# adaLN's remaining groups after both mixers, and the state-space recurrence over chunks on VectorE

## The chip, the core and the metric

The kernel runs on one core of a Trainium2 chip. The core has five engines that each work through a queue of their own, in order: TensorE (PE in the profile; its weight loads are PEld), VectorE (DVE), ScalarE (ACT), GpSimd (POOL) and SyncE (SP), which here issues nearly all transfers. The metric is the device time of one execution in microseconds.

## The reference

One layer of a streaming encoder for 512 tokens of width 2048, all in 32-bit floats:

```python
mod = (silu(c) @ w_ada + b_ada)                      # 2048 -> 6 x 2048
sh_m, sc_m, g_m, sh_f, sc_f, g_f = split(mod, 6)
h = layer_norm(x) * (1 + sc_m) + sh_m
u, q, k, v, z, beta, a, gate_s, gate_g = split(h @ w_in)
y_s = s5_mixer(u, ...) @ w_up_ssm                    # 64 groups x 16 channels, 64 complex states each
y_g = gated_deltanet(q, k, v, z, beta, a, ...) @ w_up_gdn   # 8 heads, chunks of 64 tokens
m = sigmoid(gate_s) * y_s + sigmoid(gate_g) * y_g
x = layer_norm(alpha * x + g_m * (m @ w_out), ln1_g, ln1_b)
h = layer_norm(x) * (1 + sc_f) + sh_f
x = layer_norm(alpha * x + g_f * swiglu(h), ln2_g, ln2_b)
```

The state-space mixer (S5) is a linear recurrence over the tokens. The delta-rule mixer (gated DeltaNet, "gd") goes head by head and, inside a head, chunk by chunk.

## The kernel before

**Stages.** PE runs one main line of matrix products: the input tiles for u, then for each of eight heads its q, k, v and z tiles with two gate tiles ahead of each head but the first, the remaining gate tiles, the GLU, the two up projections (merge), the output projection in two token halves, and the feed-forward layer in groups of 8 hidden tiles. Each weight block of 512 KB is loaded by SP into `raw` (three buffers), split by ACT into `whi` and by DVE into `wlo` (both 32-bit in a form PE multiplies in one pass), and each product is three PE instructions: high by high, high by low, low by high.

**Side lines.** The mixers, the adaLN sums and the LayerNorms are Python generators woven into the main line by `Order`: it keeps a rough price for each instruction, and after each triple of products (`tick`) it emits the next piece of any side line whose inputs should be there by then. Only the order of each engine's queue comes of this; on the chip each engine waits for what its next instruction needs. Where the main line can't go on, `until(...)` emits pieces of the side lines with no products between. The places used below: ahead of the tiles of head h it asks for `heads_done >= h - 1`; at the end of the output projection it drains the first half's LayerNorm line.

**The state-space mixer** (`s5_batch`, eight batches). POOL makes tables V and H (names s_V, s_W, s_H), PE makes the chunks' contributions, ACT brings them to `St` (s_S), and then the recurrence over chunks runs in `cstep`: 14 steps of four dependent POOL instructions in each batch, seven of them on 64 columns and seven on 8. POOL then adds the carried states (s5wf), and PE forms the output from s_K and s_H (px_s).

**The delta-rule mixer.** `gdn_prep` makes a head's decays on POOL and ACT (g_G, g_E, g_ET); `gdn_solve` inverts its triangular matrix on PE and DVE (g_T, g_X, g_TT), walks over four pairs of chunks (vn, St), and closes the head: squares on ACT, so on DVE, ro on POOL, g_th on DVE, then four closing transposes on PE (px_gd<-cst,g_th).

**adaLN.** The shift and scale of the first LayerNorm are made at the start. The other four vectors are `ada_rest()`: 16 groups of 512 columns, each 16 loads of 256 KB (SP) and 16 multiply-adds into `aacc` on DVE, then a few small products on PE (px_ada). The line is added as soon as the heads' conv weights are there, so it runs beside the mixers, and it only takes DVE when `Order` holds DVE for free. `ada_line` also has a second form, used when the buffers of `P2` exist, that is, after the mixers: five of the 16 products go to ACT, four sums to POOL into `aacc2`, and one more DVE sum joins the two. With `ada_deep` six loads are in flight instead of four. In this kernel all 16 groups are emitted before `P2` exists.

`switch()` waits for both mixers, frees their memory and opens `P2` (pools bp and q2); it runs between two pairs of gate tiles. The gate row for the output projection (`ada_m`, 4 groups), the columns for the second LayerNorm (`ada_f`, 12 groups) and the last row (`ada_done`, 16 groups) are asked for later.

Of the kernel before, what the change touches and what calls it, by code (L numbers as in the profile page):

```python
# [16 lines left out]
PSUM = bass.MemoryType.PSUM  # L17
# [19 lines left out]
def shape_constants():  # L37
    """128-wide masks, then masks of 64 x 64 diagonal blocks, stacked twice over the partitions."""
    i = np.arange(128)[:, None]
    j = np.arange(128)[None, :]  # L40
    m = [np.eye(128), j < i, i <= j, i // 16 == j // 16]
    i, j = i % 64, np.arange(64)[None, :]
    pair = (i // 2 == j // 2)
    m += [i == j, -1.0 * (pair & (j < i)), -1.0 * (pair & (i < j))]
    m += [(i // b == j // b + 1) & (i // b % 2 == 1) for b in (2, 4, 8, 16, 32)]
    return np.concatenate([a.astype(np.float32) for a in m], axis=1)
# [10 lines left out]
class Order:  # L57
    """Emission order of all engines: a main line of matrix products with side lines woven in.

    A rough model of the engines tells when each result is there, so that a side line's next piece is emitted  # L60
    about when its inputs are.
    """
    LAT = 0.12
# [12 lines left out]
    def _first(self, ap):  # L76
        """When the slot of a tile that is written for the first time gets free."""
        t = ap.tensor
        nm = ap.name
        if nm in self.ready or not hasattr(t, "tag_meta") or t.tag_meta is None:  # L80
            return 0.0
        q = self.slots.setdefault(t.tag, [])
        q.append(nm)
        n = t.tag_meta.bufs
        return self.last.get(q[-n - 1], 0.0) + self.LAT if len(q) > n else 0.0
# [73 lines left out]
class Engine:  # L159
    """An engine's instructions, with their rough price told to the order."""  # L160

# [110 lines left out]
def s5_setup(k, p, lam_re, lam_im, log_dt):  # L272
    """Powers of the discretised poles and their B factors, in [(re|im, state), group] and [(group parity, state), pair]."""
    nc, v, act, pool, pe = k.nc, k.v, k.act, k.pool, k.pe
# [98 lines left out]
def s5_batch(k, j, prm, d_col):  # L373
    """One tile of 128 channels (8 groups): u^T comes from k.du, 2 * gelu(y)^T goes to k.dz."""
    v, act, pool, pe, ld = k.v, k.act, k.pool, k.pe, k.ld
    b_re, b_im, c_re, c_im = prm
    s, t = k.s5, k.t5
# [84 lines left out]
    def cstep(dst, prev, rr, rs, n):  # L462
        x = w1[:, :, :, 0:n]
        shp = [128, 4, 2, n]
        for src, cf_ in ((prev, bc(rr.unsqueeze(2).unsqueeze(3), shp)), (prev[:, :, ::-1], bc(rs.rearrange("p r q -> p q r").unsqueeze(3), shp))):
            pool.tensor_tensor(out=x, in0=src, in1=cf_, op=M)
            pool.tensor_tensor(out=dst, in0=dst, in1=x, op=A)
    a8r, a8s = s.R8[:, 0, 0, q0:q0 + 4], s.R8s[:, :, q0:q0 + 4]
# [59 lines left out]
def gdn_setup(k, p, psb, a_log, dt_bias, conv_w, norm_w):  # L528
    """psb rows 0..7: beta logits, rows 8..15: decay logits, over tokens."""
    v, act, pool, pe, ld = k.v, k.act, k.pool, k.pe, k.ld  # L530
# [76 lines left out]
def gdn_conv(k, h, which, ps):  # L607
    """Causal convolution over tokens, out of PSUM."""
    s = k.gd
    a = k.tg("qkv"[which])  # L610
    col = lambda w: s.cw[:, 24 * w + 8 * which + h:24 * w + 8 * which + h + 1]
    k.act.activation(a, ps, AF.Identity, scale=col(3))
    for w in (2, 1, 0):
        d = 3 - w
        k.v.scalar_tensor_tensor(out=a[:, d:512], in0=ps[:, 0:512 - d], scalar=col(w), in1=a[:, d:512], op0=M, op1=A)
    return a
# [21 lines left out]
def gdn_prep(k, h):  # L638
    """All of a head that does not wait for the chunks before: decays, norms, the strictly lower matrix, q k^T."""
    v, act, pool, pe = k.v, k.act, k.pool, k.pe  # L640
# [106 lines left out]
def gdn_solve(k, h, r):  # L747
    """The inverse of the unit lower matrix by doubling blocks, then the chunks' recurrence and the head's output."""
    v, act, pool, pe = k.v, k.act, k.pool, k.pe
# [136 lines left out]
class Weights:  # L886
    """The stream of weight blocks, loaded and split into two float32r parts ahead of their use."""

# [63 lines left out]
    def poll(self):  # L952
        """The next block's load, once its slot is free."""
        i = self.loaded
# [7 lines left out]
def kernel(ctx, tc, x, c, w_ada, b_ada, w_in, lam_re, lam_im, log_dt, b_re, b_im, c_re, c_im,  # L962
# [39 lines left out]

# [1 line left out]
    ws = Weights(k, wpool)  # L1004
# [47 lines left out]

# [1 line left out]
    cst = cpool.tile([128, 128], F32, name="cst")  # L1054
# [18 lines left out]
    def by_pos(a):  # L1073
        """A tile whose tokens are ordered by their position in the chunk first, read in the tokens' order."""
        return a.rearrange("p (s c) -> p c s", s=8)

# [1 line left out]
    def split(hi, lo, src, eng=None):  # L1078
# [8 lines left out]
    def after(first):  # L1087
        """Between products: the next block's split and the side lines."""
        if first:
            ws.run_ahead()  # L1090
        o.tick()
# [11 lines left out]
    def gemm2(kt, acts, done, pre=None):  # L1103
        """Two neighbouring 128-column tiles, K in blocks of 8 slices."""
        pss = [psum_mm(), psum_mm()]
# [17 lines left out]
    def ada_line(p, col0):  # L1123
        """Per-partition partial sums of 512 adaLN columns."""
        acc = p.tile([128, 512], F32, name="aacc", tag="aacc", bufs=1)
# [34 lines left out]
    def ada_cols_line(p, j, q, dst, plus):  # L1160
        """512 columns of adaLN vector j, as columns."""
        acc = yield from ada_line(p, 2048 * j + 512 * q)
# [6 lines left out]
    def ada_row_line(p, j, q):  # L1169
        """Half of 512 columns of adaLN vector j, to a row in DRAM."""  # L1170
        acc = yield from ada_line(p, 2048 * j + 512 * q)
# [10 lines left out]

# [1 line left out]
    hT = []  # L1184
# [158 lines left out]

# [1 line left out]
    adp = ctx.enter_context(pool_of(name="adp", bufs=1, side="right"))  # L1345
# [15 lines left out]

# [1 line left out]
    gps, sps = ExitStack(), ExitStack()  # L1363
# [32 lines left out]
    o.until(lambda: k.cw_ready)  # L1396
    o.add(ada_rest())
    gate_next = iter(range(0, 32, 2))
# [7 lines left out]
    for h in range(8):  # L1406
# [9 lines left out]
        k.heads[h, 3] = z  # L1416
# [1 line left out]
    def switch():  # L1418
        """The mixers' memory becomes the operands' of the later products."""
        o.drain(s5l)  # L1420
# [22 lines left out]
        k.ada_deep = True  # L1443
        o.add(operands())

    def bt(dtype=F32R):
# [17 lines left out]

# [1 line left out]
    k.ada_deep = False  # L1466
# [62 lines left out]
    def row_of(src, q):  # L1529
        """A quarter of a row of 2048, on all partitions."""  # L1530
        return row_to(P2[1].tile([128, 512], F32, name="grow", tag="grow", bufs=1), src, q)
# [4 lines left out]

# [1 line left out]
    xa = [[None] * 4 for _ in range(4)]  # L1538
    h2 = [[None] * 16 for _ in range(2)]

    def ln_stats(st):
        """Mean, rstd and -mean * rstd of a token tile, as columns."""
        mv = cpool.tile([128, 2], F32, name="mv", tag="mv", bufs=4)
# [13 lines left out]
    def affine(r, st, g, b, how):  # L1557
        """((r - mean) * rstd) * g + b, in place; how: 0 on DVE, 1 shared, 2 without DVE."""
        if how == 0:
# [7 lines left out]
    def ln_half(hf, new_big):  # L1567
        """LN1, then LN0 with the FFN's adaLN, for 256 tokens; alpha * x1 stays in xa, h2^T goes to h2[hf]."""
        rows = []
# [84 lines left out]

# [1 line left out]

    def ffn_tile(gsj, hs):
        """2 * silu(gate) * up of one hidden tile, for the token halves hs."""
        pss = []
# [25 lines left out]
    def scaled(t, q, ps, gf):  # L1685
        """Adds the second gate's row times a product to a tile of the residual."""
        tmp = t2("ld")
# [33 lines left out]

# [1 line left out]
    k.gf_rows += [row_to(bt(F32), drow[5], q) for q in range(2, 4)]  # L1723
# [71 lines left out]
```

## Time and profile before

| | |
|---|---|
| median of 3 runs | 3234.25 us (3231.43 to 3240.14) |
| span of the profiled execution | 3234.4 us |
| busy, PE / DVE / ACT / POOL | 96% / 49% / 29% / 27% |
| mean granted clock of PE | 0.973 |
| moved by DMA | 458.6 MB, 142 GB/s |

The profile is of one execution. Its span, from the first to the last instruction, is 3234.4 us; no other time of that execution is given, and the span lies within 0.2 us of the median. Each row of a group gives the engine, the operation, output <- inputs by the program's names, the shape, the count, then busy us and mean ns of one, then the idle time before it and what ended that. A row "PE a <- DVE b" says that PE waited, before an instruction that writes a, for DVE to write b. Nearly all elementwise code goes through one helper (L170), so groups are told apart by tile names.

Behind the mixers, by the table of stretches, come the gates, the GLU and the merge (to about 1520 us), the output projection with the first LayerNorm half (to about 1700 us) and the feed-forward layer.

### The profile page before, as it was taken

To read this page: it belongs to the slowest core of one execution; us is meant where nothing else is said; L and a number is where in the kernel's file an instruction comes from. 1 tells how busy PE (TensorE), PEld (TensorE's weight loads), DVE (VectorE), ACT (ScalarE), POOL (GpSimd) and SP (SyncE) were. 2 spreads that over 40 slices of the span, in tenths; PEclk is the share of its full clock that TensorE was granted. 3 is DMA by queue.
4 is the path that set the end of the run, shared out by engine and by line. 5 is a ranking of instruction groups with operands and counts; after the bars stand their busy time and mean duration, and the time that the engine had idled before them with its cause. 6 is when DMAs were issued, how large, how long until landed. Compare 5 with 4: busy or idle time off the path is not lost.

```text
span 3234.4 us, 47422 instructions
## 1 busy us (share of the span) xinstructions
PE 3093.7 (96%) x19409; PEld 2699.8 (83%) x19409; DVE 1596.2 (49%) x2023; ACT 923.6 (29%) x1306; POOL 871.3 (27%) x1125
## 2 busy tenths in 40 slices
PE   6899999988999999999999999999999999999997
PEld 3587777877777788888879999998998999899895
DVE  6546776756866432444677543333233333333327
ACT  3233332222232232322354532221221222222121
POOL 4747766656754100000031102002001100200202
PEclk8899999988999999999999999999999999999998
DMA  9655556545555244445767543333333333333333
GB/s 342 213 147 156 151 162 181 151 138 169 162 143 175 79 156 134 152 147 163 237 209 202 160 150 105 92 95 108 92 92 105 98 92 98 104 93 95 108 98 117
DMA packets 521754, 458.60 MB, mean 142 GB/s; under 512 B 56144, under 2 KB 403632, under 8 KB 521536
## 3 DMA queue, kind: packets, MB, share of 16 engines
q1 hardware_dynamic: 514336, 442.47, 44.9%
q10 hardware_dynamic: 7200, 13.10, 1.1%
q8 instruction: 152, 2.49, 0.3%
q14 instruction: 66, 0.54, 0.1%
HBM read 435.60 MB, written 19.89 MB: 141 GB/s over the span
## 4 chain that ended last, share of the span: by engine, by line
PE 69%; POOL 9%; issue 5%; DVE 5%; DMA 2%; ACT 2%; SPq 1%; POOLq 0%; DVEq 0%; ACTq 0%
PE pm L211 51%; PE px_fo L211 14%; POOL s_S L170 3%; POOL s5w L170 2%; PE px_gd L211 2%; DVE aacc L170 1%; PE px_s L211 1%; SPq L170 1%; DMA w<-in_w_ada_dram 1%; DVE wlo L170 1%; DVE at L170 1%; ACT whi L170 1%; POOL g_E L170 1%; POOL g_ET L170 1%; POOL s_H L170 0%
## 5 line engine op out<-in xcount | busy, mean ns | idle before, releaser
L170 DVE TENSOR_TENSOR wlo<-raw,whi 128x1024 fp32r<-128x1024 f32 x541 | 684.0, 1266 | 899.8 <-ACT whi L170 896.8
L211 PE MATMUL pm<-at,whi 128*128 128x512 f32 (+1 forms) x3200 | 986.2, 379 | 6.4 <-ACT whi L170 3.6
L211 PE MATMUL pm<-bt,whi 128*128 128x256 f32 (+1 forms) x5312 | 988.5, 291 | 0.3 <-ACT whi L170 0.3
L170 ACT CAST whi<-raw 128x1024 fp32r<-128x1024 f32 x541 | 566.1, 1048 | 1098.6 <-PE pm L211 538.9
L211 PEld LDWEIGHTS pm<-bt,whi 128*128 128x128 f32 x5312 | 800.9, 192 | 15.9 <-ACT whi L170 0.5
L211 PEld LDWEIGHTS pm<-at,whi 128*128 128x128 f32 x3200 | 591.2, 192 | 102.9 <-ACT whi L170 4.0
L211 PE MATMUL pm<-bt,wlo 128*128 128x256 f32 (+1 forms) x2656 | 632.1, 291 | 1.5 <-DVE wlo L170 1.5
L211 PE MATMUL pm<-at,wlo 128*128 128x512 f32 (+1 forms) x1600 | 594.9, 372 | 2.5 <-DVE wlo L170 2.5
L211 PEld LDWEIGHTS pm<-bt,wlo 128*128 128x128 f32 x2656 | 447.5, 192 | 9.5 <-DVE wlo L170 1.9
L170 POOL TENSOR_TENSOR at<-at,ld 128x512 f32<-128x512 f32 x80 | 120.5, 1537 | 1148.7 <-DVE ld L170 1148.7
L211 PEld LDWEIGHTS pm<-at,wlo 128*128 128x128 f32 x1600 | 306.5, 192 | 55.9 <-DVE wlo L170 3.3
L211 PE MATMUL px_fo<-whi,at 128*128 128x512 f32 x976 | 304.7, 389 | 1.7 <-ACT whi L170 1.7
L170 DVE SCALAR_TENSOR_TENSOR aacc<-w,ccol,aacc 128x512 f32<-128x512 f32 x240 | 217.5, 906 | 26.6 <-DMA w<-in_w_ada_dram 22.4
L211 PEld LDWEIGHTS px_fo<-whi,at 128*128 128x128 f32 x976 | 183.2, 188 | 39.9 <-ACT whi L170 2.1
L211 PE MATMUL px_fo<-wlo,at 128*128 128x512 f32 x488 | 190.0, 389 | 0.8 <-DVE wlo L170 0.8
L170 POOL TENSOR_TENSOR rs<-rs,mhalf 128x1 f32<-128x1 f32 (+1 forms) x13 | 11.4, 873 | 627.8 <-DVE rs L170 627.8
L170 POOL TENSOR_TENSOR s_S<-s_S,s5w 128x64 f32<-128x64 f32 (+1 forms) x224 | 106.9, 477 | 17.6
L211 PEld LDWEIGHTS px_fo<-wlo,at 128*128 128x128 f32 x488 | 91.7, 188 | 19.9 <-DVE wlo L170 1.1
L211 PE MATMUL pm<-whi,bt 128*128 128x512 f32 x320 | 103.2, 396 | 3.3 <-DVE at L170 3.3
L211 PE MATMUL px_fo<-whi,bt 128*128 128x512 f32 x320 | 101.8, 389 | 0.0
L170 DVE SCALAR_TENSOR_TENSOR gs<-gg,pm 128x512 f32<-128x512 f32 x36 | 24.7, 687 | 154.4 <-ACT gg L170 154.4
L170 DVE TENSOR_TENSOR gs<-gs,pm 128x512 f32<-128x512 f32 x36 | 24.7, 687 | 132.5 <-PE pm L211 132.5
(374 smaller groups left out, 3139.1 us busy)
## 6 DMA issues: line engine op xcount, KB each, us to landing
raw<-in_ffn_w_in_dram SPq DMA_DIRECT2D x208, 512.0 KB, 4.1
raw<-in_w_in_dram SPq DMA_DIRECT2D x146, 512.0 KB, 3.8
w<-in_w_ada_dram SPq DMA_DIRECT2D x256, 256.0 KB, 3.6
raw<-in_ffn_w_out_dram SPq DMA_DIRECT2D x88, 512.0 KB, 3.6
wad<-in_w_ada_dram SPq DMA_DIRECT2D x64, 512.0 KB, 5.6
raw<-in_w_mix_out_dram SPq DMA_DIRECT2D x64, 512.0 KB, 4.4
raw<-in_w_up_gdn_dram SPq DMA_DIRECT2D x16, 512.0 KB, 3.4
raw<-in_w_up_ssm_dram SPq DMA_DIRECT2D x16, 512.0 KB, 3.4
```

What stands on the lines that cost most here:

```text
L170: r = f(*a, **kw)
L211: r = self.e.matmul(out, **kw)
```

## The change

Two edits do something; all the others take comments and docstrings out.

```diff
@@ s5_batch, cstep
         for src, cf_ in ((prev, ...), (prev[:, :, ::-1], ...)):
-            pool.tensor_tensor(out=x, in0=src, in1=cf_, op=M)
-            pool.tensor_tensor(out=dst, in0=dst, in1=x, op=A)
+            v.tensor_tensor(out=x, in0=src, in1=cf_, op=M)
+            v.tensor_tensor(out=dst, in0=dst, in1=x, op=A)
@@ ahead of the loop over heads
     o.until(lambda: k.cw_ready)
-    o.add(ada_rest())
     gate_next = iter(range(0, 32, 2))
@@ switch()
         k.ada_deep = True
         o.add(operands())
+        o.add(ada_rest())
```

The 448 instructions of the recurrence (8 batches x 56) go from POOL's queue to DVE's. The adaLN groups start after `switch()`, so they now take `ada_line`'s second form. Because all side lines share one plan, the order moves in many other places too. Three of them follow.

PE's queue where head 0 ends, before: the four closing transposes stand among products of the main line (pm<-at), and so do the tables of the next state-space batch (px_s).

```order
L216 MATMUL px_s_3360<-cst,s_V 128x128 x4
L211 MATMUL px_s_3368<-s5Cs,s_V 128x128 x4
L211 MATMUL pm<-at,whi 128x512 x2
L211 MATMUL pm<-at,wlo 128x512
L211 MATMUL px_s_3386<-s5Cs,s_V 128x128 x4
L216 MATMUL px_gd<-cst,g_th 128x128 x4
L211 MATMUL pm<-at,whi 128x512 x2
L211 MATMUL pm<-at,wlo 128x512
```

The same place in PE's queue now, in two pieces: the last two chunk steps of head 0, and, after 16 small products of the state-space mixer (px_s<-s_U,s_K and px_s<-s_X,s_H in turn, of which the first and the last two are shown), the closing transposes.

```order
L211 MATMUL px_gd<-vn,g_kt 128x128
L211 MATMUL pm<-vn,g_ET 128x128
L211 MATMUL px_gd<-g_v,TTfull 128x128
L211 MATMUL px_gd<-St,g_wT 128x128
L211 MATMUL pm<-St,g_G 128x128
L211 MATMUL pm<-vn,g_ET 128x128
L211 MATMUL px_s_3170<-s_U,s_K 128x64
```

```order
L211 MATMUL px_s_3170<-s_U,s_K 128x64
L211 MATMUL px_s_3170<-s_X,s_H 128x64
L216 MATMUL px_gd<-cst,g_th 128x128 x4
L211 MATMUL px_gd<-g_T,g_MT 64x64 x8
L211 MATMUL pm<-at,whi 128x512 x2
L211 MATMUL pm<-at,wlo 128x512
```

No main product is left between the last chunk step and the transposes: this is the `until` ahead of the tiles of head 2, and the same holds, with zero, one or ten triples of products between, at the `until` ahead of each of the heads 3 to 7. Before, each head ended some way ahead of its `until`.

DVE's queue in the output projection's second half, before (at<-at,mv,gg and at<-at,rs,gs are the first LayerNorm's affine step, BN_STATS its statistics, pm<-pm,grow the gate row's product):

```order
L170 BN_STATS st<-at 128x6
L170 SCALAR_TENSOR_TENSOR at<-at,mv,gg 128x512
L170 SCALAR_TENSOR_TENSOR at<-at,rs,gs 128x512
L170 TENSOR_TENSOR wlo<-raw,whi 128x1024 x2
L170 BN_STATS st<-at 128x6
L170 TENSOR_TENSOR pm<-pm,grow 128x512
L170 SCALAR_TENSOR_TENSOR at<-at,pm 128x512
```

The same place in DVE's queue now:

```order
L170 SCALAR_TENSOR_TENSOR at<-at,mv,gg 128x512
L170 SCALAR_TENSOR_TENSOR at<-at,rs,gs 128x512
L170 SCALAR_TENSOR_TENSOR aacc<-w_12971,ccol,aacc 128x512
L170 TENSOR_TENSOR wlo<-raw,whi 128x1024
L170 SCALAR_TENSOR_TENSOR aacc<-w_12979,ccol,aacc 128x512
L170 TENSOR_TENSOR wlo<-raw,whi 128x1024
L170 SCALAR_TENSOR_TENSOR aacc<-w_13000,ccol,aacc 128x512
L170 TENSOR_TENSOR pm<-pm,grow 128x512
```

An adaLN multiply-add (aacc) now stands before most weight splits (wlo). By the order, about ten of the 16 groups end before the output projection, and the last ends in the first feed-forward tiles.

PE's queue where the output projection ends (pm<-whi,bt) and the feed-forward tiles begin (pm<-bt,whi, 256 columns), now:

```order
L211 MATMUL pm<-wlo,bt 128x512
L211 MATMUL pm<-whi,bt 128x512
L216 MATMUL px_tr<-cst,ld 128x128 x16
L211 MATMUL pm<-bt,whi 128x256 x2
L211 MATMUL pm<-bt,wlo 128x256
```

The 16 transposes (px_tr) are the last half of the first LayerNorm half's; before, all 32 stood in fours among the output projection's products, and the first feed-forward tile followed the last product directly. At the second half's end 16 stand in a row now, where 12 did before.

## The prediction

> **What bounds the kernel now.** I read the page from the top: busy time, the slices with the granted clock, then a table of stretches, then who TensorE (PE) waits for, then the moments of the longest waits.
>
> ```profile
> PE 3093.7 (96%) x19409; PEld 2699.8 (83%) x19409; DVE 1596.2 (49%) x2023; ACT 923.6 (29%) x1306; POOL 871.3 (27%) x1125
> PEclk8899999988999999999999999999999999999998
> core 0: us, PE busy (x) PEld busy (x) DVE busy (x) ACT busy (x) POOL busy (x), PEclk, DMA share, GB/s
> 160.00:1120.00 960.00, 895.42 (x5856) 739.40 (x5856) 625.49 (x926) 288.09 (x530) 571.47 (x825) 0.95 0.52 152
> 1200.00:1520.00 320.00, 320.00 (x1413) 264.96 (x1413) 135.94 (x149) 92.99 (x110) 0.00 (x0) 1.00 0.46 146
> 1520.00:1760.00 240.00, 231.50 (x1240) 198.56 (x1239) 169.62 (x214) 110.41 (x136) 40.01 (x27) 0.99 0.69 219
> 1760.00:1840.00 80.00, 75.03 (x608) 74.51 (x607) 44.12 (x63) 48.75 (x77) 15.39 (x9) 0.96 0.56 161
> 780.00:800.00 20.00, 16.64 (x81) 14.20 (x81) 9.65 (x14) 4.08 (x8) 5.11 (x4) 0.63 0.39 108
> ...
> 783.36 0.69 PE L211 MATMUL px_s<-s_X,s_H 128*128 128x64 f32 x2 [8.57 <-POOL s_H L170]
> ```
>
> PE is busy 96% of the span, so time can be won only where it idles or where its clock is low. The table says where: between 160 and 1120 us, with both mixers running beside the input projection, PE idles 960 - 895.4 = 64.6 us and is granted 0.95 of its clock. What it loses there is about 960 - 895.42 x 0.95 = **109 us**: each us of idle time drags 109 / 64.6 = 1.69 us along, because a pause pulls the granted clock down (0.63 over the 20 us around the longest wait, 8.57 us for s_H; last two rows). Between 1200 and 1520 us (gates, GLU, merge) nothing is lost, and a product of 512 columns takes 320 / 1413 = 0.226 us. Around the output projection (1520 to 1760 us) the loss is 240 - 231.5 x 0.99 = 10.8 us.
>
> What PE waits for in the mixers' stretch, total us, times, longest:
>
> ```profile
> PE px_s L211 <- POOL s_H L170: 14.4, 3, 8.6
> PE px_gd L211 <- DVE g_T L170: 9.6, 3, 4.6
> PE px_gd L211 <- DVE g_X L170: 7.8, 4, 3.8
> PE px_gd L211 <- ACT g_th L170: 7.4, 2, 5.0
> PE px_ada L211 <- DVE aacc L170: 6.2, 4, 5.1
> PE px_gd L211 <- POOL g_T L170: 5.1, 1, 5.1
> PE px_gd L216 <- DVE g_th L170: 3.5, 1, 3.5
> PE px_gd L211 <- POOL s_X L170: 1.9, 1, 1.9
> ACT g_G L170 <- POOL g_ET L170: 43.6, 8, 8.2
> ```
>
> GpSimd (POOL) is behind most of it: s_H, g_T and s_X directly, and the two g_th rows because ScalarE (ACT) stands before g_G until POOL has made g_ET (last row, 8.2 us at most), with the tanh behind it in its queue. aacc is the adaLN sum itself.
>
> **The change, part by part.** *The recurrence leaves POOL.* Its 448 instructions are these groups:
>
> ```profile
> L170 POOL TENSOR_TENSOR s_S<-s_S,s5w 128x64 f32<-128x64 f32 (+1 forms) x224 | 106.9, 477 | 17.6
> L170 POOL TENSOR_TENSOR s5w<-s_S,R 128x64 f32<-128x64 f32 (+1 forms) x112 | 47.5, 424 | 79.7 <-ACT s_S L170 72.4
> L170 POOL TENSOR_TENSOR s5w<-s_S,R8s 128x64 f32<-128x64 f32 x56 | 26.8, 479 | 4.4
> L170 POOL TENSOR_TENSOR s5w<-s_S,R64s 128x8 f32<-128x8 f32 x56 | 20.7, 370 | 4.4
> L170 DVE TENSOR_TENSOR gt<-g_G,gcol 128x4 f32<-128x4 f32 x8 | 1.3, 164 | 3.6 <-DMA g_G<-dG 3.6
> L170 DVE SCALAR_TENSOR_TENSOR St<-St,gl,px_gd 128x128 f32<-128x128 f32 x16 | 5.5, 342 | 6.9 <-PE px_gd L211 6.9
> 160.00:1120.00 960.00, 17.27 (x80) 11.45 (x80) 238.44 (x288) 4.58 (x8) 0.95 0.52 152
> ```
>
> POOL gives up 106.9 + 47.5 + 26.8 + 20.7 = 202 of its 571 us. On VectorE (DVE) no such instruction stands in the trace; the nearest are one of 4 columns at 164 ns and one of 128 columns at 342 ns, so 448 cost 73 to 153 us. I take about 100, as the widths are 64 and 8. None of it is on PE's path by itself.
>
> *adaLN leaves the mixers.* The last row above is the table of stretches for the tile aacc alone (PE, PEld, DVE, ACT): 288 DVE instructions go, 238 us, so DVE falls from 625 to about 625 - 238 + 100 = 487 us in the stretch although it takes on the recurrence. The waits that hang on POOL's lateness or on aacc go: 14.4 + 7.4 + 6.2 + 5.1 + 3.5 + 1.9 = 38.5 us, with the slow clock 38.5 x 1.69 = **-65 us**. At least nothing is won; at most the whole 109. The waits for DVE's g_T and g_X (17.4 us) stay.
>
> *New waits.* By the order of instructions, six times PE now reaches the point at which head h - 1 must be done (h = 2 to 7) with that head's end still in its queue: four times the last chunk's product and the head's closing transposes have at most one triple of products between them (0.7 us), twice they have ten triples (30 x 0.226 = 6.8 us). Behind the waiting transposes stand the next head's products and all weights. How long the head's end takes is seen twice here, quiet and busy:
>
> ```profile
> 1139.73 0.38 PE L211 MATMUL pm<-vn,g_ET 128*128 128x128 f32 x2
> 1142.72 0.69 DVE L170 TENSOR_TENSOR g_th<-pm,ro 128x512 f32<-128x512 f32 x1 [1.13 <-POOL ro L170]
> 826.43 0.38 PE L211 MATMUL pm<-vn,g_ET 128*128 128x128 f32 x2
> 834.21 0.68 DVE L170 TENSOR_TENSOR g_th<-pm,ro 128x512 f32<-128x512 f32 x1
> ```
>
> From the product's end to g_th's end: 1143.4 - 1140.1 = 3.3 us, and 834.9 - 826.8 = 8.1 us. I take 5 us, nearer to the quiet one since no other line is fed at that point, for four heads, and nothing for the two that are covered: 4 x 5 x 1.69 = **+34 us**. Ends: 4 x 3.3 x 1.69 = 22, and 6 x 8.1 x 1.69 = 82 if the cover is eaten by engines that are still behind.
>
> *adaLN where it lands.* 16 groups of 16 loads start after the mixers and end, by the order, in the first FFN tiles; about ten of them fall before the output projection, where PE, DVE (136 of 320 us), ACT (93) and transfers (share 0.46) leave room, so I cost them at nothing; each is 16 x 256 KB = 4.2 MB, and by the order some 141 products (32 us) lie between the ends of two. The SyncE queue carries them between the weight blocks, which are loaded three ahead. The other six fall into 1520 to 1760 us.
>
> ```profile
> L170 DVE SCALAR_TENSOR_TENSOR aacc<-w,ccol,aacc 128x512 f32<-128x512 f32 x240 | 217.5, 906 | 26.6 <-DMA w<-in_w_ada_dram 22.4
> w<-in_w_ada_dram SPq DMA_DIRECT2D x256, 256.0 KB, 3.6
> raw<-in_w_mix_out_dram SPq DMA_DIRECT2D x57, 512.0 KB, 4.4
> 1631.22 0.79 PE L211 MATMUL pm<-wlo,bt 128*128 128x512 f32 x1 [1.97 <-DVE wlo L170]
> 1803.12 0.47 PE L216 MATMUL px_tr<-cst,ld 128*128 128x128 f32 x1 [4.73 <-ACT ld L170]
> L170 POOL TENSOR_TENSOR at<-at,ld 128x512 f32<-128x512 f32 x80 | 120.5, 1537 | 1148.7 <-DVE ld L170 1148.7
> ```
>
> Of each group of 16, five products now go to ACT and four sums to POOL, eleven stay on DVE with one sum: 12 x 0.9 = 10.5 us or a little more. Six groups add 63 us to DVE's 169.6 of 240: 233, hardly any slack, and the weights' low parts (wlo), for which PE waits up to 1.97 us there, queue among them. Transfers rise by 6 x 4.2 MB / 240 us = 105 to 324 GB/s, a share of 0.69 x 324 / 219 = 1.02, which is no slack either. I take two and a half times the present 10.8 us, +18 with blocks that land late included (ends 0 and the rival below). And the first LayerNorm half is no longer done when the output projection ends: 16 transposes in a row stand there in PE's queue. The same row of transposes stands at the second half today and costs 80 - 75.03 x 0.96 = 8 us (the wait at 1803.12 is its core): +8. Together **+26 us**.
>
> The sum: -65 + 34 + 26 = -5 us on the profiled execution's 3234.4 us, which is the median of the runs (3234.25) within 0.2: **3229 us**.
>
> **The rivals.** *All of it is won (0.27).* With POOL and DVE lighter the heads' ends take 3.3 us, the g_T and g_X waits go too (17.4 x 1.69 = 29), and behind the mixers only the 8 us are paid: -65 - 29 + 22 + 8 = -64, 3170 us. For it speaks that POOL stood behind most waits; against it that g_T waits when DVE's split stretches beside POOL's s_H, which stays.
>
> *The heads' ends become the bound (0.17), slower.* At 8.1 us each, all six uncovered, they cost 82 instead of 34: 3277 us. From 8.1 down it decides as soon as the four bare ones take (65 - 26) / 1.69 / 4 = 5.8 us each. For it: s_H's three instructions stand on POOL just before the ro that closes the head.
>
> *DVE overflows in the output projection (0.10), slower.* POOL's 24 sums of 1.54 us would hold up DVE's two-input work by 37 us: 233 + 37 = 270 in 240, 30 x 1.69 = 51 instead of 18, 3262 us. It decides once the overflow passes some 14 us.
>
> *Nothing is relieved (0.06).* DVE and POOL hold each other up, so that the recurrence is as slow as before, only elsewhere:
>
> ```profile
> 778.01 2.01 POOL L170 TENSOR_TENSOR s_W<-PAi,s5Cs 128x1024 f32<-128x1024 f32 x1
> 778.41 2.69 DVE L170 TENSOR_TENSOR wlo<-raw,whi 128x1024 fp32r<-128x1024 f32 x1 [5.98 <-ACT whi L170]
> 780.10 3.20 POOL L170 TENSOR_TENSOR s_H<-s_H,s_W 128x1024 f32<-128x1024 f32 x1
> L170 DVE TENSOR_TENSOR wlo<-raw,whi 128x1024 fp32r<-128x1024 f32 x541 | 684.0, 1266 | 899.8 <-ACT whi L170 896.8
> ```
>
> A split of 1.27 us takes 2.69 beside POOL's. If 448 DVE instructions took POOL's present 202 us, half of the 65 would come back: 3262 us. The Trainium skill, "GPSIMD Engine Reference", section "8. Key points", says so of the interface: GpSimd shares it with VectorE and contends with instructions of two SBUF inputs, which all 448 are; the rows above agree.
>
> **How the numbers follow.** My forecast, 3214 to 3244 by itself, gets 0.40: of it 0.11 is faster, 0.27 within and 0.02 slower by the bound of 0.3% (9.7 us), about what a measurement can tell from no change. With the first rival faster has 0.38, same 0.27; slower is 0.02 + 0.17 + 0.10 + 0.06 = 0.35. The range, 3182 to 3278 us, leaves out the far part of the first rival and what lies beyond the long heads' ends.
>
> **What would show it.** In the table of stretches POOL should fall to about 370 us in the mixers and DVE to about 490; the rows for s_H, aacc and POOL's g_T should shrink to a few us. Six waits of px_gd for g_th (or px_s for s_H), 3 to 6 us each, should stand some 90 us apart. The groups of the recurrence on DVE should lie at 0.16 to 0.34 us. Between 1200 and 1520 us PE should stay at 320; DVE should pass 90% around the output projection, and one wait of px_tr for ld near its end should be new. I am wrong if PE loses time in the gates or the merge, if the heads' ends do not make PE wait, or if the recurrence on DVE holds up the splits.

## The result and the profile after

| | before | after |
|---|---|---|
| median, runs of the same chip | 3236.34 us (4 runs) | 3250.81 us (4 runs, 3247.14 to 3255.97) |
| ratio, with its 95% interval | | 1.0053 [1.0033, 1.0072] |
| span of the profiled execution | 3234.4 us | 3245.4 us |
| mean granted clock | 0.973 | 0.975 |

The changed kernel is 0.5% slower. The page of the profile after, its busy times and clock, then its table of stretches (the same stretches and columns as before; PE is now further ahead in the program at each of these times):

```profile
PE 3091.2 (95%) x19409; PEld 2692.9 (83%) x19409; DVE 1653.5 (51%) x2407; ACT 976.2 (30%) x1386; POOL 752.6 (23%) x741
PEclk9899999999999999998899999999999999999998
160.00:1120.00 960.00, 941.74 (x6200) 784.05 (x6199) 534.38 (x1120) 317.23 (x566) 355.79 (x382) 0.99 0.35 99
1200.00:1520.00 320.00, 303.65 (x1319) 248.23 (x1318) 235.05 (x270) 115.16 (x141) 54.98 (x34) 0.97 0.78 255
1520.00:1760.00 240.00, 190.55 (x929) 156.51 (x929) 176.20 (x229) 98.28 (x133) 62.12 (x41) 0.90 0.74 232
1760.00:1840.00 80.00, 74.39 (x575) 72.94 (x574) 52.32 (x76) 49.13 (x78) 19.95 (x13) 0.93 0.55 155
```

The totals hide the story: PE's busy time is what it was (3091 against 3094 us). The slices of the clock show it: the two 8s that stood in the mixers (slices 9 and 10) are gone, and two new ones stand at slices 19 and 20, which are 1460 to 1623 us. In the mixers PE now runs 6200 products in the 960 us, not 5856, and loses 960 - 941.74 x 0.99 = 28 us there, not 109. In 1520 to 1760 us it loses 240 - 190.55 x 0.90 = 69 us, not 11.

Fixed stretches compare different work once one kernel is ahead. So the table below takes other marks: PE runs the same 15,792 weight products in the same order in each kernel, and the start of the next one behind the 432nd, 2640th, 4464th, 5232nd and 6000th marks the end of the input tiles, the heads, the merge, the output projection and the first eight FFN tiles (first token half). Times in us, worked out from the records of PE:

| | before | after | difference |
|---|---|---|---|
| up to the heads | 225.0 | 219.7 | -5.3 |
| heads | 856.4 | 753.9 | -102.5 |
| gates, GLU and merge | 431.2 | 449.8 | +18.6 |
| output projection | 188.2 | 263.9 | +75.7 |
| first FFN half tiles | 104.5 | 129.1 | +24.6 |
| the rest | 1429.2 | 1429.1 | -0.1 |
| span | 3234.4 | 3245.4 | +11.0 |

The heads won 102.5 us, of which 18.6 were only moved: PE is busy for 449.7 of the 449.8 us after them at a clock of 1.00, and runs 142 products more there than before, small ones of the mixers and of adaLN. So the heads to the merge won **84 us** and the next two stages lost **100 us**. The part up to the heads took 218 to 226 us in the executions below without a pattern; I count its 5 us as scatter of the start.

What PE waited for in the mixers' stretch, after (total us, times, longest):

```profile
PE px_s L216 <- DMA s5C<-in_ssm_c_im_dram: 8.2, 5, 2.8
PE px_gd L211 <- ACT g_th L170: 4.8, 2, 4.2
PE px_gd L216 <- DVE g_th L170: 3.6, 2, 1.9
PE px_s L216 <- POOL s_V L170: 1.4, 1, 1.4
PE pm L211 <- DVE vn L170: 0.2, 1, 0.2
```

The rows for s_H, aacc, POOL's g_T and DVE's g_T and g_X are all gone. The eight rows of PE that the prediction shows add up to 56 us; all of PE's waits in the stretch are now 18 us.

The stretch from the merge's end to the end of the first FFN half tiles, by the table of stretches, of after:

```profile
1423.00:1816.00 393.00, 321.69 (x1634) 269.11 (x1632) 281.50 (x359) 168.57 (x230) 95.50 (x62) 0.90 0.72 225
```

and of before:

```profile
1512.00:1805.00 293.00, 279.53 (x1603) 244.70 (x1602) 200.94 (x260) 146.06 (x194) 54.24 (x36) 0.99 0.67 209
```

The same products take 100 us more, and neither DVE (281.5 of 393 us) nor the transfers (a share of 0.72) fill the stretch. The waits in it, after: SyncE's queue, then ACT, then PE:

```profile
SPq L170 <- DVE wlo L170: 83.9, 37, 6.4
SPq L170 <- POOL aacc L170: 67.1, 19, 8.7
SPq L170 <- DVE aacc L170: 48.4, 34, 7.5
...
ACT whi L170 <- DMA raw<-in_w_mix_out_dram: 110.0, 39, 9.6
ACT whi L170 <- DMA raw<-in_ffn_w_in_dram: 29.5, 11, 9.7
...
PE pm L211 <- ACT whi L170: 22.3, 10, 4.9
PE pm L211 <- DVE at L170: 18.8, 5, 5.0
PE pm L211 <- DVE wlo L170: 18.3, 21, 3.0
PE px_tr L216 <- ACT ld L170: 11.7, 6, 5.8
```

Before, the same three:

```profile
SPq L170 <- DVE wlo L170: 149.5, 76, 6.2
...
ACT whi L170 <- DMA raw<-in_w_mix_out_dram: 35.8, 20, 4.9
...
PE px_tr L216 <- ACT ld L170: 5.0, 2, 4.7
PE pm L211 <- DVE wlo L170: 4.9, 4, 2.0
PE pm L211 <- DVE at L170: 3.3, 3, 1.3
```

Read from the bottom up: PE waits for both parts of the weights (whi, wlo) and for DVE to empty its accumulators (at). ACT, which makes whi, waits three times as long for weight blocks to land (110 against 36 us). SyncE, which loads them, used to wait mostly for the weights' own slots (wlo) and never for an adaLN load; now it stands 67.1 + 48.4 = 115 us, nearly all of it before adaLN loads whose slot a sum on POOL or DVE has not yet read. The queue is in order, so the weight loads behind such a load wait too. That was my theory going into the experiments; its rivals were the bytes (the DMA engines' share went from 0.67 to 0.72 over these stages) and the sums' work, which stands ahead of the splits in the queues of DVE and ACT.

### The profile page after: what moved, and what is told of

Same layout as the page of the kernel before. It is cut to its first block, busy times and chain, and to the rows that moved or that the text cites. A ratio compares the mean times of both kernels' runs of the same rounds, so it can differ in the third digit from the quotient of the medians.

```text
span 3245.4 us, 47489 instructions
## 1 busy us (share of the span) xinstructions
PE 3091.2 (95%) x19409; PEld 2692.9 (83%) x19409; DVE 1653.5 (51%) x2407; ACT 976.2 (30%) x1386; POOL 752.6 (23%) x741
## 4 chain that ended last, share of the span: by engine, by line
PE 79%; DMA 7%; DVE 6%; POOL 3%; issue 2%; SPq 2%; ACT 2%; ACTq 0%; DVEq 0%; POOLq 0%
PE pm L211 57%; PE px_fo L211 14%; PE px_gd L211 4%; DMA raw<-in_w_mix_out_dram 3%; PE px_s L211 2%; SPq L170 2%; DVE aacc L170 2%; DVE wlo L170 1%; DMA raw<-in_ffn_w_in_dram 1%; DVE at L170 1%; ACT whi L170 1%; POOL eq L170 1%; DVE acc L170 1%; DMA w<-in_w_ada_dram 0%; PE px_u L211 0%
## 5 line engine op out<-in xcount | busy, mean ns | idle before, releaser
L170 POOL TENSOR_TENSOR aacc<-aacc,w 128x512 f32<-128x512 f32 x59 | 96.5, 1636 | 417.5 <-ACT w L170 417.4
L170 DVE SCALAR_TENSOR_TENSOR aacc<-w,ccol,aacc 128x512 f32<-128x512 f32 x148 | 154.0, 1041 | 10.9 <-DMA w<-in_w_ada_dram 9.3
L211 PE MATMUL pm<-whi,bt 128*128 128x512 f32 x320 | 109.9, 416 | 20.0 <-DVE at L170 18.8
L211 PE MATMUL pm<-whi,at 128*128 128x512 f32 x224 | 81.7, 434 | 14.9 <-ACT whi L170 14.9
L211 PEld LDWEIGHTS pm<-whi,bt 128*128 128x128 f32 x320 | 64.1, 200 | 36.6 <-DVE at L170 21.2
```

Source lines behind the costliest of these rows:

```text
L170: r = f(*a, **kw)
L211: r = self.e.matmul(out, **kw)
```

## The experiments

All fifteen in one table. The ratio is to the kernel before, run on the same chip beside it; stages are by the marks above, from one profiled execution, and the stages of before are those of one execution on one chip. The rest behind the first FFN half tiles is 1428.2 to 1429.5 us in all of them. The eight kernels with the recurrence on DVE and adaLN behind the mixers have the same code from the heads to the merge but for small shifts of order, and lie within 3.6 us there; differences of that size between stages say nothing.

| kernel | median us | ratio [95% interval] | heads to merge | output projection + first FFN half tiles |
|---|---|---|---|---|
| before | | 1 | 1287.6 | 292.6 |
| after | 3250.8 | 1.0053 [1.0033, 1.0072] | 1203.7 | 392.9 |
| e1_rec_only | 3209.2 | 0.9948 [0.993, 0.9966] | 1264.2 | 290.1 |
| e2_ada_only | 3283.0 | 1.0174 [1.0156, 1.0193] | 1250.3 | 379.3 |
| e3_pool_queue | 3211.4 | 0.9956 [0.994, 0.9972] | 1205.1 | 356.1 |
| e4_half_bytes | 3247.5 | 1.0064 [1.0046, 1.0081] | 1202.2 | 391.6 |
| e5_short_sums | 3205.8 | 0.9907 [0.9889, 0.9924] | 1205.8 | 348.2 |
| e8_pool_half | 3212.5 | 0.9933 [0.9918, 0.9948] | 1202.7 | 354.3 |
| e9_loads_only | 3188.1 | 0.9869 [0.9846, 0.9892] | 1205.2 | 328.2 |
| e10_sums_only | 3192.1 | 0.9881 [0.9858, 0.9903] | 1205.3 | 337.4 |
| e13_neither | 3158.2 | 0.9771 [0.9753, 0.979] | 1203.9 | 306.8 |
| e7_from_head2 | 3215.3 | 0.9945 [0.9928, 0.9962] | 1270.8 | 292.1 |
| e14_from_head3 | 3222.7 | 0.9965 [0.9952, 0.9978] | 1277.4 | 291.9 |
| e6_from_head4 | 3195.0 | **0.9881** [0.9866, 0.9895] | 1250.3 | 290.6 |
| e11_from_head5 | 3210.1 | 0.9936 [0.9916, 0.9956] | 1264.1 | 291.1 |
| e12_head5_pool | 3230.6 | 1.0002 [0.9988, 1.0015] | 1282.8 | 290.7 |
| e15_head4_early_c | 3210.2 | 0.9932 [0.9912, 0.9951] | 1263.8 | 292.5 |

### Each edit alone

The recurrence alone (e1), on the kernel before:

```diff
-            pool.tensor_tensor(out=x, in0=src, in1=cf_, op=M)
-            pool.tensor_tensor(out=dst, in0=dst, in1=x, op=A)
+            v.tensor_tensor(out=x, in0=src, in1=cf_, op=M)
+            v.tensor_tensor(out=dst, in0=dst, in1=x, op=A)
```

> The recurrence over chunks on VectorE alone; the adaLN groups stay beside the mixers as before. If POOL's lateness caused the mixers' waits (my theory), POOL falls to about 370 us in 160 to 1120 us, DVE rises to about 740 of 960, the waits for s_H, POOL's g_T and g_ET go (31 us, with the slow clock some 50), the output projection stays at the 188 us of before, and the time is about 3185 us. If the adaLN groups' leaving was what freed the mixers, DVE at 740 us makes PE wait for g_T, g_X and the weights' low halves, and the time is 3230 us or more.

The move of adaLN alone (e2): the changed kernel with these two lines put back on POOL.

> The changed kernel with the recurrence back on GpSimd, so only the adaLN groups are moved. My theory: the loss in the output projection and the first FFN half tiles (about 105 us) belongs to the move alone, so the output projection takes some 260 us as in the changed kernel, the mixers win only a part (the waits for aacc and some of DVE's, 10 to 50 us), and the time is 3285 to 3330 us. If the recurrence on DVE has a share in that loss, the output projection is shorter, and the time is at or below the changed kernel's 3251 us.

The recurrence alone wins: 0.9948. Its 23 us in the heads to the merge are half of the 50 I expected. The move alone loses: 1.0174. It wins 37 us in the mixers and loses 87 behind the merge. So most of the loss belongs to the move: 87 of the 100 us come without the recurrence on DVE (379 us there, and 393 with it), and the recurrence alone loses nothing there (290.1 us in e1). The last 14 us come only with both edits; their cause stays open, since the order of the queues differs between e2 and the changed kernel. The time of e2, 3283 us, lies 2 us below the range I had expected. In the mixers the two together win 84 us, more than 23 + 37 = 60: with one of the two in place the heads still wait for the engine that has it (in 160 to 1120 us PE's waits name DVE in e1, with 15.5 us for g_th, 8.4 for g_X and 7.7 for vn, and POOL in e2, with 13.5 us for g_T).

### The queue or the bytes

e3 is the changed kernel with the adaLN loads on GpSimd's queue; PE, DVE and ACT run the same instructions in the same order (`o.run` tells the plan the price of a step, so that it does not shift).

```diff
-            k.sync.dma_start(out=raw, in_=w_ada[...])
+            nc.gpsimd.dma_start(out=raw, in_=w_ada[...])
+            o.run("s", 0.06, raw, [src], 0.05 + raw.nbytes() / 345e3)
```

> The changed kernel with the adaLN loads issued on GpSimd's queue in place of SyncE's; PE, DVE and ACT run the same instructions in the same order. Queue theory: an adaLN load that waits for its slot's readers no longer holds up the weight blocks behind it; the SyncE waits for aacc (103 us between 1423 and 1690 us) go, ACT waits for the output projection's blocks fall from 110 us to about the 36 of before, and most of the 76 + 25 us come back: 3155 to 3190 us. Bandwidth theory (the transfers' share of 0.74 makes the blocks late): the same bytes in the same time, 3240 to 3260 us. Split theory (the weights' splits stand behind the adaLN sums in the queues of DVE and ACT): the same orders, 3240 to 3260 us.

e4 leaves the queue alone and cuts the bytes (r4 and v4 read 128 columns four times over, so the modulation is made from other data; the order on DVE and PE shifts in places):

```diff
-            k.sync.dma_start(out=raw, in_=src)
+            m = 512 if acc2 is None or len(raws) % 3 == 1 else 128
+            nc.sync.dma_start(out=raw[:, 0:m], in_=src[:, 0:m])
...
-                v.scalar_tensor_tensor(out=acc, in0=raws[kt], scalar=sc, in1=acc, op0=M, op1=A)
+                v.scalar_tensor_tensor(out=v4(acc), in0=r4(raws[kt]), scalar=sc, in1=v4(acc), op0=M, op1=A)
```

> The changed kernel in which the adaLN groups behind the mixers read only 128 of the 512 columns of 11 of their 16 blocks and repeat them, so the modulation is computed from other data; the instructions, their widths and the queue stay, and the groups' bytes fall to 48%. Bandwidth theory: the share of the DMA engines between 1423 and 1690 us falls from 0.73 to about 0.55, the blocks land in time, and half or more of the 100 us come back: 3200 us or less. Queue theory: a load still waits at the head of SyncE's queue until its slot's readers are done, so little comes back: 3230 to 3251 us. Split theory: 3240 to 3260 us.

With half the bytes nothing changes (391.6 against 392.9 us behind the merge). With the other queue 37 of the 100 us come back, and the kernel beats the one before (0.9956), though not by as much as I had expected. In e3, between the merge's end and the end of the first FFN half tiles (1427 to 1783 us), SyncE and ACT wait for:

```profile
SPq L170 <- DVE wlo L170: 212.5, 79, 18.4
...
SPq L170 <- DVE aacc L170: 7.5, 4, 2.4
...
ACT whi L170 <- DMA raw<-in_w_mix_out_dram: 54.1, 26, 8.6
```

The waits for aacc are nearly gone from SyncE (7.5 us), which is back to standing before the weights' own slots, as before the change; ACT's wait for blocks has halved. The Trainium skill, "Trainium Kernel Development and Optimization", section "Key Constraints", says that transfers issued from SP, ACT and POOL share the same 16 DMA engines, and that issuing from several only saves the sequencer's issue time. Here it saved more than that: a queue in order also passes on the wait of the load at its head, 115 us of it in these stages.

The edit changes a second thing with it. The page of e3 has the adaLN bytes (256 loads, 67 MB) under a transfer queue of their own, where the changed kernel has them with the weights under q1:

```profile
q1 hardware_dynamic: 477472, 375.34, 37.7%
q0 software_dynamic: 20480, 67.13, 6.2%
```

No run separates this from the order of issue. What speaks for the order is that a weight block that has been issued is hardly faster: by the records of issue and landing, the 59 blocks of the output projection issued in these stages take 5.5 us on average in e3, 5.8 in the changed kernel and 4.8 before.

### What is left with the other queue

Two runs on top of e3. In e5 the sums on DVE are short, in e8 the bytes are halved as in e4.

```diff
-                v.scalar_tensor_tensor(out=acc, in0=raws[kt], scalar=sc, in1=acc, op0=M, op1=A)
+                n = 512 if acc2 is None else 128
+                nc.vector.scalar_tensor_tensor(out=acc[:, 0:n], in0=raws[kt][:, 0:n], scalar=sc, in1=acc[:, 0:n], op0=M, op1=A)
```

> The loads on GpSimd's queue as in e3_pool_queue, and the adaLN groups' own sums on DVE (scalar times block plus sum) take only the first 128 of 512 columns, so most of the modulation is left out; the order on every engine stays. Split theory (what e3 still loses against before, 48 us in the output projection and 16 in the first FFN half tiles, is the weights' splits and LayerNorm steps standing behind the sums on DVE): some 85 sums of 0.9 us shrink to about 0.35, 15 to 40 us come back, 3170 to 3195 us. Bandwidth theory: the bytes are the same, 3205 to 3215 us.

> The loads on GpSimd's queue as in e3_pool_queue, and 11 of 16 blocks of an adaLN group read only 128 of their 512 columns and repeat them (modulation from other data), so their bytes fall to 48%. Bandwidth theory for the rest of the loss (share of the DMA engines 0.84 and 0.76 in the two halves of the output projection): 20 to 50 us come back, 3160 to 3190 us. Split theory: 3205 to 3215 us.

Each run came out where the other theory had put it. Shorter sums on DVE gave 8 us of the 64 that e3 still loses, halved bytes 2; by the ratios of the whole kernels, which ran on another chip than e3, it is 16 and 7. Either way, neither DVE's time in the sums nor the number of bytes is by itself most of what costs there. The sums on ACT and POOL kept their length.

### Loads, sums, or neither

So the next three took one whole side away from the changed kernel, on SyncE's queue as it stands. e9 loads all blocks and adds up only the first two of a group; e10 makes all sums and loads only the first four or six blocks of a group; e13 does neither beyond the first two blocks. TensorE's instructions and their order are those of the changed kernel in all three.

```diff
@@ e9, ada_line
+            if acc2 is not None and kt > 1:
...
+                    o.run("v", 0.2 + 512 * 0.00105, acc, [r, sc])
...
@@ e10, load
+            if acc2 is not None and len(raws) >= depth:
...
+                raws.append(raws[len(raws) - depth])
...
+                return
```

> The changed kernel, SyncE's queue, all 256 adaLN blocks loaded as before, but of each group behind the mixers only the first two blocks are added up, so the modulation is left incomplete; TensorE runs the same instructions in the same order. Slots come free as soon as a load has landed, so the queue holds nothing up long; what stays is the transfers themselves. If the transfers cost what e3_pool_queue and e8_pool_half left over (some 55 of the 100 us), the time is 3195 us or more. If the sums' work on DVE, ACT and GpSimd costs it, nearly all of the 100 us come back: 3145 to 3170 us.

> The opposite: all sums are made, in the same order on all four engines, but behind the mixers only the first four or six blocks of a group are loaded and then read again, so the modulation is made from other data. No load stands in SyncE's queue for long, and a quarter to a third of the bytes is left. If the sums' work costs what GpSimd's queue left over, the time is like e3_pool_queue or a little less: 3190 to 3212 us. If transfers do, 3145 to 3170 us.

> The changed kernel with neither: behind the mixers only the first two blocks of an adaLN group are loaded and added up (the modulation is left incomplete); TensorE's instructions and their order stay. If loads, sums and their coupling through SyncE's queue are the whole of the 100 us that the changed kernel loses in the output projection and the first FFN half tiles, these stages are back at about 293 us but for the row of transposes (+8), and the time is 3150 to 3165 us. If the order itself costs more (LayerNorm's steps and the products of ones placed differently), 3170 us or more.

Against the 292.6 us of before, the output projection and the first FFN half tiles take

| adaLN behind the mixers | lost there, us |
|---|---|
| neither loads nor sums (e13) | 14 |
| loads alone (e9) | 36 |
| sums alone (e10) | 45 |
| both, loads on GpSimd's queue (e3) | 64 |
| both, loads on SyncE's queue (after) | 100 |

The 14 us are the order itself, with the two blocks of a group that are left; its largest wait stands where the first LayerNorm half is now drained in a row (timeline of e13; the same wait is 5.84 us in the changed kernel):

```profile
1628.93 0.47 PE L216 MATMUL px_tr<-cst,ld 128*128 128x128 f32 x1 [5.04 <-ACT ld L170]
```

Loads add 36 - 14 = 21 us and sums 45 - 14 = 31 us. 14 + 21 + 31 = 66 us, close to what both cost when the loads do not stand in SyncE's queue (64). The other 34 to 37 us go when the adaLN loads leave that queue, in which a late sum can hold up a load, and that load a weight block. The sum is a reckoning and not a proof that the parts simply add: the loads of e9 are still in SyncE's queue, which stands before them until earlier ones have landed:

```profile
SPq L170 <- DMA w<-in_w_ada_dram: 28.4, 26, 4.9
```

So the 21 us hold some queueing as well as transfers. What in the sums costs the 31 us, when shorter sums on DVE gave back so little, stays open too. Of the expectations, e13 (3158 us) came as written, e10 (3192 us) as written if the sums count, and e9 (3188 us) fell between its two cases: loads and sums both have a share, and neither is the whole.

What the coupling looks like in the changed kernel, at one place of the output projection. The first row is SyncE's wait before an adaLN load, which ends at 1625.9 us; then come the way of a weight block behind it, from its issue to its landing, the split on ACT and the product on PE (start and length, us):

```profile
SPq L170 <- POOL aacc L170: 5.3, 1, 5.3
...
1628.56 8.00 DMA raw<-in_w_mix_out_dram
...
1636.66 1.04 ACT L170 CAST whi<-raw 128x1024 fp32r<-128x1024 f32 x1 [9.15 <-DMA raw<-in_w_mix_out_dram]
...
1637.76 0.50 PE L211 MATMUL pm<-whi,at 128*128 128x512 f32 x1 [3.22 <-ACT whi L170]
```

The 8.00 us are counted from the issue, so they are no time in SyncE's queue: this block is late because it was issued late and because it was long on its way. The seven longest pieces of the chain that ended last, in the output projection, are all such ways of weight blocks, 7.0 to 8.3 us each; before, the longest way of one of these blocks was 7.1.

### Where to start the adaLN groups

If the groups cost only where they meet the output projection, they should start before the mixers end. With the recurrence on DVE, `ada_rest()` is added ahead of a head's tiles in place of `switch()`:

```diff
     for h in range(8):
+        if h == 4:
+            o.add(ada_rest())
...
         o.add(operands())
-        o.add(ada_rest())
```

> The changed kernel with the adaLN groups started at the fifth of the eight heads, not behind both mixers; by the order of instructions their last product then comes before the merge is over. My theory (the recurrence on DVE frees the mixers; the adaLN groups cost only where they meet the output projection): the output projection is back at about 188 us and the first FFN half tiles at 104, the mixers keep most of the 90 us won, 3150 to 3185 us. If adaLN beside the heads is what hurt the mixers, half or more of the 90 us go there and the time is 3195 us or more.

> As e6_from_head4, started at the third head. The output projection as in before (188 us). With all groups but a few beside the heads, DVE carries about 650 to 690 us of the mixers' 960, so by my theory some 15 to 30 us more are lost there than with a start at the fifth head: 3165 to 3200 us. If DVE's load in the mixers does not matter, the same as e6_from_head4.

> The adaLN groups started at the fourth head, between e7_from_head2 (3215 us) and e6_from_head4 (3195). If the place counts smoothly, 3200 to 3210 us.

> As e6_from_head4 with the adaLN groups started one head later, so that the gates and the merge, where DVE is busy 136 of 320 us in the kernel before, take one or two groups more. By the order the last group ends just before the output projection. The mixers lose less than with the fifth head (42 us there against the changed kernel), the output projection stays at about 190 us: 3178 to 3195 us. If the groups in the merge run over into the output projection, 3195 to 3210 us.

In all four the output projection and the first FFN half tiles are back at 291 to 292 us, which confirms that their loss comes only where the groups meet them. The best, from the fifth head, is 0.9881 of the kernel before, 1.2% faster, and the fastest of the kernels that compute everything. But the mixers keep only 37 of their 84 us there, and the place does not count smoothly: 3215, 3223, 3195 and 3210 us for a start at heads three to six. All four came out above what I had expected. One reason for the last is plain: a group that is still open when the gates end makes PE wait, in one piece (timeline of e11_from_head5):

```profile
1255.05 1.84 PE L211 MATMUL px_ada<-one,aacc 128*128 128x1 f32 x8 [13.94 <-DVE aacc L170]
```

### Queues beside the heads

In e6_from_head4 PE's largest wait in the mixers was for the matrices C, whose small loads I took to be held up by adaLN loads on SyncE:

```profile
PE px_s L216 <- DMA s5C<-in_ssm_c_im_dram: 18.2, 7, 4.7
PE px_gd L216 <- DVE g_th L170: 6.6, 4, 2.5
```

Two ways around it: all adaLN loads on GpSimd's queue (e12, on e11), or the small loads one batch ahead (e15, on e6):

```diff
@@ e15, s5_batch
...
+    B, Cin = k.pre5.pop(j, None) or s5_load(k, g0, prm)
...
     powers(V, bb, slice(7, None, -1), A)
     yield
+    if j < 7:
+        k.pre5[j + 1] = s5_load(k, g0 + 8, prm)
```

> As e11_from_head5, with the adaLN loads on GpSimd's queue. In e6_from_head4 TensorE waited 18.2 us for the mixer's C matrices, whose loads stand behind adaLN loads on SyncE's queue (8.2 us in the changed kernel); by the queue theory that goes, and the time is 5 to 20 us below e11_from_head5. If GpSimd, which now issues 256 loads between its own work, holds up the heads, it is above it.

> As e6_from_head4, with the state-space mixer's B and C matrices of the next batch loaded one batch ahead, in front of the adaLN loads that they stood behind. TensorE's waits for them (18.2 us there) shrink to a few us; with the slow clock 10 to 25 us are won: 3170 to 3187 us. If another wait takes their place, 3190 to 3200 us.

Both are misses: 20 us slower than e11, and 15 us slower than e6. In e12, GpSimd's own waits between 600 and 1250 us:

```profile
POOL w L1138 <- DVE aacc L170: 140.6, 89, 11.8
```

POOL now stands 141 us before adaLN loads whose slot DVE has not read, and whatever the heads want of POOL next stands behind them. It is the same blocking in another queue; behind the mixers POOL had little that was urgent, here it has the heads' steps. That this is the whole of the 20 us was not tested by itself. From the heads to the merge, the wait of PE that grew most is px_ada for the sums themselves, 28.2 us where e11 has 19.0. Nor was there much to win: the wait for C is 8.9 us in e11 already and 9.0 in e12, as in the changed kernel (8.2), where no adaLN load stands beside the heads. So the theory that adaLN loads on SyncE cause that wait is not borne out; why e6 has 18.2 stays open.

In e15 the C matrices no longer stand among PE's large waits, and others do (over the whole execution):

```profile
PE px_gd L216 <- DVE g_th L170: 13.4, 4, 4.3
...
PE px_gd L211 <- DVE g_X L170: 10.1, 3, 4.7
PE px_ada L211 <- DVE aacc L170: 9.5, 6, 4.2
PE px_gd L211 <- DVE g_T L170: 9.3, 5, 2.9
```

All four are DVE's. The edit also shifts the plan of all side lines, so e15 does not show whether DVE would have been late anyway; that stays open, and so does why the four starting places differ by 28 us.

## Why the prediction was wrong

The sum was -65 + 34 + 26 = -5 us. The profiled execution gave -84 for the first two terms together, +100 for the third and -5 of start-up scatter: +11 (the medians lie 14.5 us apart). That the result lies as near the forecast as it does is luck: two large errors nearly cancel.

*First term, -65 for the waits that hang on POOL or aacc: right in kind, too small.* The mixers' loss fell from 109 to 28 us, and the heads to the merge won 84. POOL fell to 356 us as said (370). I had kept DVE's waits for g_T and g_X (17.4 us); they went too, as the first rival had it. One row counted as going stayed in good part, PE's for ACT's g_th (4.8 of 7.4 us), although ACT's wait for POOL's g_ET fell from 43.6 to 13.3 us; POOL's lateness was at most a part of that one. The 448 instructions on DVE lie where the brackets put them:

```profile
L170 DVE TENSOR_TENSOR s_S<-s_S,s5w 128x64 f32<-128x64 f32 (+1 forms) x224 | 58.8, 262 | 7.7
L170 DVE TENSOR_TENSOR s5w<-s_S,R 128x64 f32<-128x64 f32 (+1 forms) x112 | 27.3, 244 | 3.7 <-ACT s_S L170 1.5
L170 DVE TENSOR_TENSOR s5w<-s_S,R8s 128x64 f32<-128x64 f32 x56 | 16.2, 290 | 2.0
L170 DVE TENSOR_TENSOR s5w<-s_S,R64s 128x8 f32<-128x8 f32 x56 | 10.9, 194 | 2.0
```

Together 113 us, against 100 predicted (73 to 153) and 202 on POOL: the rival that nothing is relieved falls with that.

*Second term, +34 for the heads' ends at the `until` points: wrong.* PE waits for g_th at two of them, 3.6 us in all, where four of 5 us were forecast. One of the two, in the timeline of after:

```profile
598.75 0.38 PE L211 MATMUL pm<-vn,g_ET 128*128 128x128 f32 x2
598.97 0.33 PE L211 MATMUL px_s<-s_U,s_K 128*128 128x64 f32 x2
...
602.26 0.39 PE L211 MATMUL px_s<-s_X,s_H 128*128 128x64 f32 x2
604.56 1.09 PE L216 MATMUL px_gd<-cst,g_th 128*128 128x128 f32 x4 [1.91 <-DVE g_th L170]
```

The head's end takes 604.56 - 599.13 = 5.4 us from the last chunk's product, about the 5 us I took. But 16 small products of the state-space mixer stand between, 3.7 us of PE. The order of instructions showed them, in the section on the change; I counted only triples of the main line as cover. The rival that the heads' ends become the bound fails for the same reason. At 1.69 us per us of wait the term would have been +6.

*Third term, +26 for adaLN behind the mixers: this is the step that failed.* It measured +100. I sized it by DVE's load and a transfers' share of 1.02, scaled up the present loss by two and a half, and added 8 us for the row of transposes. (Twelve sums of 0.9 us are 10.8 us and not 10.5; that moves DVE's 233 us by two and decides nothing.) Neither is full there (281.5 of 393 us, 0.72): the rival of an overflowing DVE was wrong in its mechanism, and its price (+51 in place of +18) still too low. The row of transposes came in its place; it is the largest wait in the 14 us that stay with loads and sums taken away. What was missing is the third resource: SyncE's queue. The prediction says that it "carries them between the weight blocks, which are loaded three ahead" and draws nothing from it, and it priced loads, sums and queue as if each ran beside the others. The runs show 14 for the order, 21 for the loads, 31 for the sums, and 34 more that are there only with all of them on SyncE's queue, where a late sum stops a load and the load a weight block. The recurrence alone costs nothing in these stages (e1), and the move without it already costs 87 of the 100 us (e2).

Of the signs I had named, POOL's fall, the recurrence's durations, full PE through gates and merge, and the new wait of px_tr came; the six waits for g_th and a DVE above 90% did not, and DVE fell in the mixers' stretch to 534 us, not to about 490, with more of the program inside that stretch. With the terms as measured, the changes that were not made are visible too: the recurrence alone is 0.5% faster, and with adaLN from the fifth head 1.2%.

## What to carry to other kernels

Before moving a stream of loads, ask for each load what its slot still waits for, and what stands behind it in the same queue: a transfer queue in order hands a late consumer's delay to every load behind it, and no busy share shows that; the queue's own waits do. Price a stage that several streams share by what couples them, not by the fullest engine: here two side effects of 21 and 31 us became 86 together. And moving a queue's wait elsewhere can cost as much as it wins where the new queue has urgent work: the same edit won 37 us behind the mixers and lost 20 beside them.

## What the runs showed of the hardware

A load issued from GpSimd occupies that engine for about half a microsecond, in e3_pool_queue:

```profile
L1138 POOL DMA_DIRECT2D w<-in_w_ada_dram x237 | 128.6, 544 | 275.1 <-DVE aacc L170 184.2 <-ACT aacc L170 70.8 <-POOL aacc L170 9.8
```

That is 128.6 us of POOL for 237 loads, beside 752.6 us that it is busy in the changed kernel.

A us that PE waits cost more than a us in both places where this case has it. Behind the merge PE's waits grew from 13.5 us (the rows of before above, and 0.3 for whi) to 71 (the four rows of after), 58 us more, and these stages grew by 100 us: 1.7 us for each us of waiting, with the granted clock at 0.90 there against 0.99. In the mixers the prediction had read 1.69 from one kernel. It is no constant: reckoned in the same way for the same stages, e3, e9 and e10 give 1.9, 2.1 and 1.8.
